# A full-row low part for the attention scores, and the convolution's shifted products all on VectorE

## The chip, the cores and the metric

One core of a Trainium2 chip runs the whole program. The metric is the device time of one execution in microseconds (us), the median of several runs. The engines are named as the profile names them: PE (TensorE matmul), PEld (its weight loads), DVE (VectorE), ACT (ScalarE), POOL (GpSimd), SP (SyncE, which issues most DMAs).

## The reference, cut to what matters

The reference is two transformer blocks in float32 over 1024 tokens of width 1024. Only two pieces of the first block are touched by the change. One is a causal depthwise convolution of width 31 over 256 channels; the other is a differential attention with 4 heads, each with two maps of 64 dimensions.

```python
u = a_val * jax.nn.sigmoid(a_gate)                       # 1024 x 256
y = conv_general_dilated(u, w_dw, padding=[(30, 0)], feature_group_count=256) + b_dw
y = silu(layer_norm(y)) @ w_pw + b_pw
...
q, k = rms_norm(q.reshape(.., 4, 2, 64)), rms_norm(k.reshape(.., 4, 2, 64))
s = einsum("bhmqd,bhmkd->bhmqk", q, k) * scale - slope * dist   # both maps m, causal
p = softmax(s)
o = einsum("bhqk,bhkd->bhqd", p[:, :, 0] - lam * p[:, :, 1], v)
```

After it come an output projection, a mixture of experts and two more layers, which the change leaves as they are.

## The kernel before, in words

Matrix products work on float32 values split into a high and a low part (`wh`, `wl` for weights, `mh`, `ml` for activations), and add three of the four partial products. A weight granule arrives by DMA in `raw` (4 buffers), ACT copies it to `wh` (L451), and `low` (L443) makes `wl`: two of three such splits go to DVE, the third to POOL (L447). Large tiles share one pool of 42 buffers, matmul results of one PSUM bank share 4 (`mm`), and the score tiles share 2 (`sc`).

The order of work on each engine follows the order in which Python generators are stepped. `_weave(main, side, steps)` takes one step of `main`, then `steps` steps of `side`. Each engine runs its own list in order, so an instruction that is traced early stands ahead of later ones on its engine. A scheduler may move an instruction behind others that it takes to be ready earlier.

The first block's stages, in order of time:

- `conv_pool`: the products for the convolution's values, its gate and the pooling input. It has 24 steps; 13 are run first, and the other 11 are the second half of the tokens (`psT`).
- `qkv`: 8 steps for V (`psV`, 24 matmuls of 512 columns each), then 24 steps for Q and K (`psQ`), in four column groups of six steps. Each Q or K tile goes through ACT (L792), DVE (`qss` L794, `qn` L797), a PE transpose, and a copy and subtraction (L813, L814). The first group's weights `wl` are split at the end of the V steps.
- `diff_attention`: 32 units (head, block of 128 queries), with scores `psD` on PE, maximum on DVE (L897), exponentials on ACT (L902), scaling on POOL (L907), combination on DVE (L908), transposes on PE (L918), then the product with V (`psO`).

`conv_taps(half)` does the 31 shifted multiply-adds of the convolution for one half of the tokens and for both channel groups `j`, in 31 steps. DVE adds all shifts of group 0 and 18 of group 1 in place (L664), 96 instructions in all. For 12 shifts of group 1, ACT makes the product (L672) and POOL adds it to a third tile `ys[2]` (L673), which POOL adds to `ys[1]` at the end (L675). Half 0 is woven into the last 11 steps of `conv_pool` at 2.6 steps each. Half 1 is the first part of the side chain of `qkv`, at 3 steps for one; `pool_out` (24 steps, with 6 wide adds on POOL, L687, and four subtractions on DVE, L693) and `conv_norm` (20 steps) come behind it in the chain.

For the scores, `k[m][h]` holds the high part of map `m` on one half of the partitions and its low part on the other half. `query_maps(h)` copies the high part of the query of each map to both partition halves, with three DMAs of 256 KB on POOL's queue: two for the tile `qh2` (L848), one in place that waits for them (L849). The matmul `high` (L876) takes 128 rows: high query with both parts of the key. The matmul `low` (L880) takes only 64 rows: low query with the high key. They follow each other in pairs, one pair for each block of at most 512 keys.

Of the kernel before, what the change touches and what calls it, by code (L numbers as in the profile page):

```python
# [10 lines left out]
F32R = mybir.dt.float32r  # L11
I32 = mybir.dt.int32
U8 = mybir.dt.uint8
AF = mybir.ActivationFunctionType
OP = mybir.AluOpType
# [242 lines left out]
def _run(g):  # L258
    for _ in g:
        pass  # L260


def _weave(main, side, steps=1.0):

    due = 0.0
    for _ in main:
        yield
        due += steps
        while due >= 1.0:
            due -= 1.0  # L270
            if next(side, _END) is not _END:
                yield
    yield from side


def _some(gen, n):

    for _ in range(n):
        if next(gen, _END) is _END:
            return  # L280
        yield


def _chain(*gens):
    for g in gens:
        yield from g
# [31 lines left out]
class _Kernel:  # L318
# [321 lines left out]
        yield from self.group(lead, [  # L640
            lambda t0, n, j=j, use=use: self.partT(("c", j), self.hm, use, t0, n=n) for j, use in enumerate(uses)])

    def conv_taps(self, half):

        nc = self.nc
        us = self.us
        if half == 0:
            self.ys = [self.d("cy") for _ in range(3)]
        ys = self.ys
        n2 = 12  # L650
        lo, hi = 512 * half, 512 * half + 512
        for j in range(2):
            nc.vector.tensor_scalar(ys[j][:, lo:hi], us[j][:, lo:hi], self.col(("cw", j), 30), self.col("cb", j),
                                    op0=OP.mult, op1=OP.add)
        if half == 0:
            nc.gpsimd.memset(ys[2][:, 0:hi], 0.0)
        else:
            nc.scalar.activation(ys[2][:, lo:hi], us[1][:, lo - 30:hi - 30], AF.Copy, scale=self.col(("cw", 1), 0))
        yield
        last = 31 if half == 0 else 30  # L660
        for sh in range(1, 31):
            a = max(lo, sh)
            for j in range(2 if sh <= 30 - n2 else 1):
                nc.vector.scalar_tensor_tensor(ys[j][:, a:hi], us[j][:, a - sh:hi - sh], self.col(("cw", j), 30 - sh),  # L664
                                               ys[j][:, a:hi], op0=OP.mult, op1=OP.add)
            n = last + n2 - 31
            if sh * n // 30 > (sh - 1) * n // 30:
                s2 = last - sh * n // 30
                a = max(lo, s2)
                p = self.t512("cpr")[:, :hi - a]  # L670
                with self.tc.issue_after(self.evicted.ins):
                    nc.scalar.activation(p, us[1][:, a - s2:hi - s2], AF.Copy, scale=self.col(("cw", 1), 30 - s2))  # L672
                nc.gpsimd.tensor_tensor(ys[2][:, a:hi], ys[2][:, a:hi], p, op=OP.add)  # L673
            yield
        nc.gpsimd.tensor_tensor(ys[1][:, lo:hi], ys[1][:, lo:hi], ys[2][:, lo:hi], op=OP.add)  # L675

    def pool_out(self):
        nc = self.nc
# [163 lines left out]

    def query_maps(self, h):

        a = self.q[0][h]
        b = self.d("qh2", dt=F32R)
        for r in (slice(0, 64), slice(64, 128)):
            self.nc.gpsimd.dma_start(b[r], a[64:128])  # L848
        self.nc.gpsimd.dma_start(a[64:128], a[0:64])  # L849
        self.q2[h] = [a, b]  # L850

    def diff_attention(self):
        nc = self.nc
# [5 lines left out]
        def unit(h, i):  # L859
# [11 lines left out]
            qa = slice(128 * i, 128 * i + 128)  # L871
            pd = {}
            blocks = [slice(c0, min(w, c0 + 512)) for c0 in range(0, w, 512)]

            def high(m, b):
                nc.tensor.matmul(pd[m][:, b], self.q2[h][m][:, qa], self.k[m][h][:, b], start=True, stop=False)  # L876

            def low(m, b):
                r = slice(64 * m, 64 * m + 64)
                nc.tensor.matmul(pd[m][:, b], self.q[1][h][r, qa], self.k[m][h][r, b], start=False, stop=True)  # L880
            for m in range(2):
                if w > 512:
                    pd[m] = self.sc("psD")
                elif m == 0:
                    both = self.sc("psD", (128, 2, 512))
                    pd = [both[:, 0], both[:, 1]]
                for b in blocks:
                    high(m, b)
                    low(m, b)
                ps = pd[m]  # L890
                if w > 512:
                    t = self.d("at")
                else:
                    if m == 0:
                        two = self.d("at", (128, 2, 512))
                    t = two[:, m]
                nc.vector.tensor_tensor_reduce(t[:, :w], ps[:, :w], bias[:, 896 - 128 * i:896 - 128 * i + w],  # L897
                                               1.0, -3.0e38, OP.add, OP.max, mx[:, m:m + 1])
                tt.append(t)
            nc.vector.tensor_scalar(nm, mx, -slope, None, op0=OP.mult)  # L900
            for m in range(2):
# [7 lines left out]
                                           op0=OP.mult, op1=OP.add)  # L909
# [20 lines left out]
            if i ^ 1 in done[h]:  # L930
                c0 = 256 * (i // 2)
                b = slice(c0, c0 + 256)
                r = q = self.t256("ar")
# [11 lines left out]
                if len(done[h]) == NT:  # L945
                    self.q[0][h] = self.q[1][h] = self.k[0][h] = self.k[1][h] = self.q2[h] = None
                yield
        yield from _pipe(unit(h, i) for h, i in ATTN_ORDER)
        self.q = self.k = self.v = None

# [1189 lines left out]
    def build(self):  # L2140
        nc = self.nc
# [26 lines left out]
        first = self.conv_pool(lead)  # L2168
        _run(_some(first, 6))
        self.lambdas()  # L2170
        _run(_some(first, 7))
        _run(_weave(first, self.conv_taps(0), 2.6))
        self.ahead = 1
        _run(_weave(self.qkv(), _chain(self.conv_taps(1), self.pool_out(), self.conv_norm()), 3))
        if self.stop == "qkv":
            return
        self.ahead = 0
# [15 lines left out]
        def products():  # L2193
            self.pre(8)
            for half, t in self.out_proj(("o1",), self.io["x"], self.after_first, order, fill, True):
                if (half, t) == (1, order[5]):
                    self.rope_tables()
                    self.make_masks()
                if (half, t) == (0, order[6]):
                    self.choose_most()  # L2200
                if (half, t) == (1, order[-1]):
                    self.ple_load(0)
                    self.pre(1)
                if (half, t) == (0, order[-1]):
                    _run(_some(side, 1))
                yield
# [75 lines left out]
```

## Time and profile before

| | |
|---|---|
| median of 3 runs | 2355.36 us (2348.99 to 2358.8) |
| the profiled execution | 2339.19 us, span 2337.4 us |
| mean granted TensorE clock in it | 0.97 |
| PE busy | 93% of the span |
| DVE busy | 65% |
| ACT busy | 50% |
| POOL busy | 23% |

The profiled execution is a single one and a little shorter than the three timed runs. Its span is the time between its first and last instruction; some 2 us lie around it. Busy shares are means over stages with different limits, and a matmul's recorded time overlaps that of its neighbours: the distance between two starts says what one costs in a row.

### The profile page before, as it was taken

The page shows a single profiled execution, that of the slowest core. Times are in us where ns is not written, and L with a number is a line of the kernel's source. Part 1 is how long each engine was busy: PE and PEld are TensorE (multiplying, and loading weights), DVE is VectorE, ACT ScalarE, POOL GpSimd, SP SyncE. Part 2 cuts the span into 40 slices and gives each one's busy share as a digit, 9 for nine tenths or more (in the row PEclk, how much of TensorE's full clock was granted, in tenths as well). Part 3 has the DMA queues.
Part 4 walks back from the last instruction along what each step waited for, and adds up shares of the span by engine and source line. Part 5 has one row for each costly group of instructions (what it writes and reads, how often), then busy time and mean ns, then how long its engine had stood idle before and what let it go on. Part 6 is the DMA issues. An engine that isn't in the chain of part 4 may idle for free.

```text
span 2337.4 us, 31235 instructions
## 1 busy us (share of the span) xinstructions
PE 2182.8 (93%) x11660; PEld 1822.4 (78%) x11660; DVE 1515.9 (65%) x2574; ACT 1171.0 (50%) x2216; POOL 531.2 (23%) x445
## 2 busy tenths in 40 slices
PE   7869999999999889988899999999998989999998
PEld 7659866787777768877687998888877777898886
DVE  5995677667777744567736775476167675676455
ACT  5414666525666656254344564266345444555344
POOL 1740033302222211012232342011012232233110
PEclk9889999999999999999999999999999999999999
DMA  5101210537899973011122014344001102103343
GB/s 202 36 1 52 80 46 24 173 117 265 241 289 317 306 224 121 10 37 46 46 81 55 19 46 162 127 181 139 27 28 41 68 30 75 42 28 126 126 154 126
DMA packets 77487, 251.95 MB, mean 108 GB/s; under 512 B 9488, under 2 KB 16784, under 8 KB 77328
## 3 DMA queue, kind: packets, MB, share of 16 engines
q1 hardware_dynamic: 65024, 205.84, 25.4%
q0 software_dynamic: 9712, 34.86, 6.3%
q10 hardware_dynamic: 2592, 9.18, 1.0%
q8 instruction: 94, 1.54, 0.3%
q14 instruction: 65, 0.53, 0.1%
HBM read 183.51 MB, written 58.98 MB: 104 GB/s over the span
## 4 chain that ended last, share of the span: by engine, by line
PE 65%; DVE 18%; ACT 6%; DMA 6%; issue 4%; POOL 1%; SPq 0%; DVEq 0%; ACTq 0%; POOLq 0%
PE psR L501 18%; PE psT L470 11%; PE psS L460 6%; PE psO L460 5%; PE psV L501 4%; DMA raw<-in_wm_dram 4%; PE psQ L501 3%; DVE cy L664 3%; PE psG L1309 2%; DVE wl L447 2%; PE psPT L1937 2%; PE psY L460 2%; DVE st L1702 2%; DVE st L1705 2%; PE psD L880 1%
## 5 line engine op out<-in xcount | busy, mean ns | idle before, releaser
L470 PE MATMUL psT<-mh,wh 128*128 128x512 f32 (+1 forms) x784 | 291.6, 372 | 10.2 <-ACT k L1570 4.4
L447 DVE TENSOR_TENSOR wl<-raw,wh 128x1024 fp32r<-128x1024 f32 x171 | 226.8, 1338 | 104.3 <-ACT wh L451 102.9
L470 PE MATMUL psT<-ml,wh 128*128 128x512 f32 (+1 forms) x784 | 288.5, 368 | 2.1 <-DVE ml L559 2.1
L470 PE MATMUL psT<-mh,wl 128*128 128x512 f32 (+1 forms) x784 | 287.2, 367 | 0.0
L451 ACT ACTIVATE wh<-raw 128x1024 fp32r<-128x1024 f32 x205 | 213.8, 1055 | 62.9 <-DMA raw<-in_wm_dram 40.5
L447 POOL TENSOR_TENSOR wl<-raw,wh 128x1024 fp32r<-128x1024 f32 x34 | 98.5, 2896 | 405.0 <-ACT wh L451 306.2
L470 PEld LDWEIGHTS psT<-mh,wh 128*128 128x128 f32 x784 | 152.6, 195 | 37.8 <-ACT k L1570 5.1
L470 PEld LDWEIGHTS psT<-ml,wh 128*128 128x128 f32 x784 | 152.8, 195 | 25.2 <-DVE ml L559 2.9
L470 PEld LDWEIGHTS psT<-mh,wl 128*128 128x128 f32 x784 | 152.5, 194 | 22.9 <-issue 0.2
L501 PE MATMUL psR<-wh,mixh 128*128 128x512 f32 x384 | 152.9, 398 | 2.7 <-DVE mpT L1942 1.7
L501 PE MATMUL psR<-wh,mixl 128*128 128x512 f32 x384 | 150.4, 392 | 0.6 <-POOL mixl L447 0.5
L501 PE MATMUL psR<-wl,mixh 128*128 128x512 f32 x384 | 150.4, 392 | 0.0
L1925 POOL TENSOR_SCALAR mp<-mp,mrr 128x512 f32<-128x512 f32 x128 | 92.1, 732 | 213.3 <-DVE mrr L1923 213.3
L1921 ACT ACTIVATE mp<-psS,mnm,rq 128x1024 f32<-128x1024 f32 x64 | 77.4, 1209 | 82.5 <-DVE mnm L1918 82.4
L501 PE MATMUL psR<-wl,mh 128*128 128x512 f32 (+1 forms) x264 | 101.3, 384 | 1.2 <-DVE wl L447 1.2
L501 PE MATMUL psR<-wh,mh 128*128 128x512 f32 (+1 forms) x264 | 102.0, 386 | 0.0
L501 PE MATMUL psR<-wh,ml 128*128 128x512 f32 (+1 forms) x264 | 101.1, 383 | 0.0
L558 ACT ACTIVATE mh<-psX 128x256 fp32r<-128x256 f32 (+1 forms) x144 | 60.8, 452 | 77.4 <-PE psX L550 72.2
L460 PEld LDWEIGHTS psO<-mpT,mv 128*128 128x128 f32 x768 | 96.4, 191 | 2.6
L1916 DVE TENSOR_REDUCE mmx<-psS 128x1 f32<-128x1024 f32 x64 | 78.0, 1219 | 29.7 <-PE psS L460 29.5
L460 PE MATMUL psO<-mpT,mv 128*128 128x256 f32 x768 | 97.1, 283 | 0.0
L664 DVE SCALAR_TENSOR_TENSOR cy<-u,cols,cy 128x512 f32<-128x512 f32 (+28 forms) x96 | 95.9, 1059 | 0.4
(496 smaller groups left out, 5723.6 us busy)
## 6 DMA issues: line engine op xcount, KB each, us to landing
raw<-in_wg_dram SPq DMA_DIRECT2D x109, 512.0 KB, 3.9
raw<-in_wm_dram SPq DMA_DIRECT2D x96, 512.0 KB, 5.3
pp<-ppo ACTq DMA_DIRECT2D x16, 512.0 KB, 7.0
h<-xr SPq DMA_DIRECT2D x16, 512.0 KB, 2.9
xr<-h SPq DMA_DIRECT2D x16, 512.0 KB, 4.4
ppr<-pp SPq DMA_DIRECT2D x16, 512.0 KB, 5.6
xt<-in_x_dram SPq DMA_DIRECT2D x8, 512.0 KB
xr<-in_x_dram SPq DMA_DIRECT2D x8, 512.0 KB, 5.0
```

The costliest lines, as they stand in the source:

```text
L447: e.tensor_tensor(out, full, high.bitcast(F32), op=OP.subtract)
L451: self.nc.scalar.activation(h, src, AF.Copy)
L460: self.nc.tensor.matmul(out, a, b, start=j == 0, stop=j == n - 1)
L470: self.nc.tensor.matmul(ps, p[:, a], q, start=k == 0 and j == 0, stop=k == nk - 1 and j == 2)
L501: self.nc.tensor.matmul(out, p, q[:, b], start=k == 0 and j == 0, stop=k == 7 and j == 2)
L558: nc.scalar.activation(h, v, AF.Copy)
L664: nc.vector.scalar_tensor_tensor(ys[j][:, a:hi], us[j][:, a - sh:hi - sh], self.col(("cw", j), 30 - sh), ys[j][:, a:hi], op0=OP.mult, op1= ...
L1309: self.nc.tensor.matmul(pg, m[x][:, k], w[:, b], start=k == 0 and n == 0, stop=k == 7 and n == 2)
L1702: nc.vector.scalar_tensor_tensor(st[(c + 1) // 8][0:64, (c + 1) % 8], st[c // 8][0:64, c % 8], er[0:64, 1, c:c + 1], ds[c % 2][0:64, c // ...
L1916: nc.vector.tensor_reduce(mx, ps, axis=AX.X, op=OP.max)
L1921: nc.scalar.activation(p, ps, AF.Exp, bias=nm, scale=self.rq[0][:, t:t + 1], accum_out=sm)
L1925: nc.gpsimd.tensor_scalar(p[:, b], p[:, b], rr, 1.0, op0=OP.mult, op1=OP.mult)
```

## The change

`conv_taps` becomes one generator for both halves. DVE does all shifted products of both groups; the products on ACT, the additions on POOL and the third tile are gone. Only 14 of its 62 steps are woven into `conv_pool`, at 1.3 for one. The other 48 are woven with `pool_out` (0.55 steps of it for one of taps), and that, followed by `conv_norm`, is woven into `qkv` at 3.4 for one.

`query_maps` now also copies the low part of the query to both partition halves, with three more DMAs and one more tile per head. The second score matmul becomes one of 128 rows: low query with both parts of the key.

```diff
-    def conv_taps(self, half):
+    def conv_taps(self):
...
-        n2 = 12
...
-            for j in range(2 if sh <= 30 - n2 else 1):
-                nc.vector.scalar_tensor_tensor(ys[j][:, a:hi], us[j][:, a - sh:hi - sh], self.col(("cw", j), 30 - sh),
-                                               ys[j][:, a:hi], op0=OP.mult, op1=OP.add)
-            n = last + n2 - 31
-            if sh * n // 30 > (sh - 1) * n // 30:
...
-                    nc.scalar.activation(p, us[1][:, a - s2:hi - s2], AF.Copy, scale=self.col(("cw", 1), 30 - s2))
-                nc.gpsimd.tensor_tensor(ys[2][:, a:hi], ys[2][:, a:hi], p, op=OP.add)
...
+        ys = self.ys = [self.d("cy") for _ in range(2)]
+        for half in range(2):
...
+            for sh in range(1, 31):
+                a = max(lo, sh)
+                for j in range(2):
+                    nc.vector.scalar_tensor_tensor(ys[j][:, a:hi], us[j][:, a - sh:hi - sh], self.col(("cw", j), 30 - sh),
+                                                   ys[j][:, a:hi], op0=OP.mult, op1=OP.add)
+                yield
...
-        a = self.q[0][h]
-        b = self.d("qh2", dt=F32R)
-        for r in (slice(0, 64), slice(64, 128)):
-            self.nc.gpsimd.dma_start(b[r], a[64:128])
-        self.nc.gpsimd.dma_start(a[64:128], a[0:64])
-        self.q2[h] = [a, b]
+        self.q2[h] = [[], []]
+        for n in range(2):
+            a = self.q[n][h]
+            b = self.d("qh2", dt=F32R)
+            for r in (slice(0, 64), slice(64, 128)):
+                self.nc.gpsimd.dma_start(b[r], a[64:128])
+            self.nc.gpsimd.dma_start(a[64:128], a[0:64])
+            for m, t in enumerate((a, b)):
+                self.q2[h][m].append(t)
...
-            def low(m, b):
-                r = slice(64 * m, 64 * m + 64)
-                nc.tensor.matmul(pd[m][:, b], self.q[1][h][r, qa], self.k[m][h][r, b], start=False, stop=True)
+            def products(m, b):
+
+                for n in range(2):
+                    nc.tensor.matmul(pd[m][:, b], self.q2[h][m][n][:, qa], self.k[m][h][:, b], start=n == 0, stop=n == 1)
...
-        _run(_weave(first, self.conv_taps(0), 2.6))
+        taps = self.conv_taps()
+        _run(_weave(first, _some(taps, 14), 1.3))
         self.ahead = 1
-        _run(_weave(self.qkv(), _chain(self.conv_taps(1), self.pool_out(), self.conv_norm()), 3))
+        _run(_weave(self.qkv(), _chain(_weave(taps, self.pool_out(), 0.55), self.conv_norm()), 3.4))
```

## Rows read from the trace of the kernel before

**Rows 1.** The page: busy time of TensorE, its share and instructions.

```profile
PE 2182.8 (93%) x11660; PEld 1822.4 (78%) x11660; DVE 1515.9 (65%) x2574; ACT 1171.0 (50%) x2216; POOL 531.2 (23%) x445
```

**Rows 2.** Windows by stage: start:end, length; busy of PE, PEld, DVE, ACT, POOL; PEclk.

```profile
97.00:150.50 53.50, 48.04 (x197) 38.65 (x195) 53.50 (x52) 18.44 (x28) 30.74 (x19) 0.90 0.09 30
150.50:174.30 23.80, 1.50 (x14) 1.30 (x12) 23.41 (x18) 0.44 (x1) 16.45 (x13) 0.60 0.00 0
174.30:240.00 65.70, 63.15 (x472) 59.65 (x473) 35.47 (x71) 31.75 (x82) 4.79 (x2) 0.96 0.19 65
240.00:289.50 49.50, 47.41 (x374) 44.77 (x374) 34.87 (x70) 36.86 (x88) 4.93 (x5) 1.00 0.24 70
289.50:425.00 135.50, 132.17 (x673) 91.67 (x671) 102.25 (x303) 93.39 (x241) 43.40 (x60) 0.97 0.12 31
```

**Rows 3.** Waits, 56 to 180 us: total, times, longest.

```profile
PE psQ L501 <- DVE wl L447: 22.3, 1, 22.3
...
PE psV L501 <- DVE wl L447: 5.5, 2, 3.2
```

**Rows 4.** Timeline of PE in the V steps: start, duration.

```profile
97.19 0.39 PE L501 MATMUL psV<-wh,ml 128*128 128x512 f32 x1
...
99.46 0.39 PE L501 MATMUL psV<-wl,mh 128*128 128x512 f32 x1
...
109.40 0.63 PE L501 MATMUL psV<-wh,ml 128*128 128x512 f32 x1
...
112.39 0.63 PE L501 MATMUL psV<-wl,mh 128*128 128x512 f32 x1
```

**Rows 5.** Windows, the shifted products (L664) alone: length, DVE busy (count), PEclk.

```profile
65.00:81.00 16.00, 15.16 (x23) 0.96 0.00 0
115.00:129.00 14.00, 14.00 (x9) 1.00 0.01 2
...
154.50:170.00 15.50, 15.25 (x8) 0.52 0.00 0
```

**Rows 6.** Timeline of POOL, the additions of half 1: start, time.

```profile
110.87 18.05 POOL L673 TENSOR_TENSOR cy<-cy,cpr 128x512 f32<-128x512 f32 x11
```

**Rows 7.** Lines, DVE from 174.3 to 289.5 us: busy us, mean ns.

```profile
L794 DVE TENSOR_REDUCE qss<-qsq 128x4 f32<-128x256 f32 x31 | 12.9, 417 | 23.2 <-ACT qsq L792 23.0
L447 DVE TENSOR_TENSOR wl<-raw,wh 128x1024 fp32r<-128x1024 f32 x6 | 9.2, 1536 | 2.7 <-ACT wh L451 2.7
L814 DVE SCALAR_TENSOR_TENSOR ql<-psQT,qg,qh 128x256 fp32r<-128x256 f32 x16 | 7.7, 481 | 1.6 <-ACT qh L813 1.2
...
L693 DVE SCALAR_TENSOR_TENSOR pd<-ps,pin 64x1008 f32<-64x1008 f32 x4 | 4.8, 1198 | 0.1
```

**Rows 8.** Timeline of PE in the attention: start, duration.

```profile
323.08 0.47 PE L876 MATMUL psD<-qh 128*128 128x512 f32 x1
323.49 0.49 PE L880 MATMUL psD<-qh,ql 64*128 64x512 f32 x1
323.91 0.38 PE L876 MATMUL psD<-ql,qh 128*128 128x256 f32 x1
```

**Rows 9.** One of the four groups of score matmuls: min/median/max ns, shapes.

```profile
L880 PE MATMUL psD<-qh,ql x48: 323/491/792, 289.9 to 416.3; 64*128 64x512 f32 x24, 64*128 64x384 f32 x8, 64*128 64x256 f32 x8, 64*128 64x128 f32 x8
```

**Rows 10.** Waits, 292 to 430 us: total, times, longest.

```profile
DVE at L897 <- PE psD L880: 19.8, 23, 2.5
...
DVE at L908 <- POOL at L907: 6.2, 9, 1.5
...
DVE few L905 <- ACT at L902: 2.6, 3, 1.2
...
DVE at L920 <- PE psAT L918: 2.2, 2, 2.0
```

**Rows 11.** Timeline of POOL: the query copies of head 0.

```profile
275.31 1.09 POOL L848 DMA_DIRECT2D qh<-qh  x2 [13.30 <-PE psQ L501]
...
282.33 0.51 POOL L849 DMA_DIRECT2D qh<-qh  x1 [4.97 <-DVE qn L797]
```

More of the change, by code (lines that the diff above doesn't have):

```diff
@@ L641, in conv_pool @@
             lambda t0, n, j=j, use=use: self.partT(("c", j), self.hm, use, t0, n=n) for j, use in enumerate(uses)])
-    def conv_taps(self, half):
+    def conv_taps(self):
         nc = self.nc
         us = self.us
-        if half == 0:
-            self.ys = [self.d("cy") for _ in range(3)]
-        ys = self.ys
-        n2 = 12
[L651 to L662, printed above, removed]
-            for j in range(2 if sh <= 30 - n2 else 1):
-                nc.vector.scalar_tensor_tensor(ys[j][:, a:hi], us[j][:, a - sh:hi - sh], self.col(("cw", j), 30 - sh),
-                                               ys[j][:, a:hi], op0=OP.mult, op1=OP.add)
-            n = last + n2 - 31
-            if sh * n // 30 > (sh - 1) * n // 30:
[L668 to L671, printed above, removed]
-                    nc.scalar.activation(p, us[1][:, a - s2:hi - s2], AF.Copy, scale=self.col(("cw", 1), 30 - s2))
-                nc.gpsimd.tensor_tensor(ys[2][:, a:hi], ys[2][:, a:hi], p, op=OP.add)
-            yield
-        nc.gpsimd.tensor_tensor(ys[1][:, lo:hi], ys[1][:, lo:hi], ys[2][:, lo:hi], op=OP.add)
@@ new lines, in conv_taps @@
+        ys = self.ys = [self.d("cy") for _ in range(2)]
+        for half in range(2):
+            lo, hi = 512 * half, 512 * half + 512
+            for j in range(2):
+                nc.vector.tensor_scalar(ys[j][:, lo:hi], us[j][:, lo:hi], self.col(("cw", j), 30), self.col("cb", j),
+                                        op0=OP.mult, op1=OP.add)
+            yield
+            for sh in range(1, 31):
+                a = max(lo, sh)
+                for j in range(2):
+                    nc.vector.scalar_tensor_tensor(ys[j][:, a:hi], us[j][:, a - sh:hi - sh], self.col(("cw", j), 30 - sh),
+                                                   ys[j][:, a:hi], op0=OP.mult, op1=OP.add)
+                yield
@@ L873, in unit @@
             blocks = [slice(c0, min(w, c0 + 512)) for c0 in range(0, w, 512)]
-            def high(m, b):
-                nc.tensor.matmul(pd[m][:, b], self.q2[h][m][:, qa], self.k[m][h][:, b], start=True, stop=False)
-            def low(m, b):
-                r = slice(64 * m, 64 * m + 64)
-                nc.tensor.matmul(pd[m][:, b], self.q[1][h][r, qa], self.k[m][h][r, b], start=False, stop=True)
+            def products(m, b):
+                for n in range(2):
+                    nc.tensor.matmul(pd[m][:, b], self.q2[h][m][n][:, qa], self.k[m][h][:, b], start=n == 0, stop=n == 1)
             for m in range(2):
@@ L887, in unit @@
                 for b in blocks:
-                    high(m, b)
-                    low(m, b)
+                    products(m, b)
                 ps = pd[m]
```

## The prediction

> **What bounds the kernel now.** The page comes first: TensorE is busy for 93% of the span [rows 1], so most of the kernel is bound by PE, and work moved among the other engines is worth something only where PE waits for one of them. The windows by stage show where that is [rows 2]. From 97 us come 53.5 us for the V steps at a mean granted clock of 0.90, and 23.8 us in which PE is busy for 1.5 us while DVE is busy for 23.4. The waits name the cause [rows 3]: PE waits once for 22.3 us and twice for 5.5 us together, each time for a low weight part `wl` from DVE. The weights have been there; the split stands on DVE behind the shifted products of half 1, which were traced before it. So in this stretch DVE sets the end.
>
> The timeline of PE gives two prices [rows 4]. At full speed (2.4 GHz) a matmul of 512 columns takes (99.46 - 97.19)/10 = 0.227 us. After the waits it takes (112.39 - 109.40)/7 = 0.427 us: PE stood, and came back at the lower level of its clock (1.2 GHz).
>
> The windows with only the shifted products show why DVE is late [rows 5]. Alone, one costs 15.16/23 = 0.66 us. From 115 to 129 us one costs 14.0/9 = 1.56 us, and from 154.5 to 170 us 15.25/8 = 1.9 us. In the earlier of these POOL was adding the products of ACT to its tile, 11 additions in 18.05 us [rows 6]; in the other it ran the wide adds of `pool_out`. A product on DVE takes two to three times as long while POOL adds.
>
> In the attention PE is the bound: busy for 132 of 135.5 us, with DVE at 102, ACT at 93 and POOL at 43 [rows 2].
>
> **The taps, removed.** 24 products on ACT and 24 additions on POOL go, which by itself gains nothing, since neither engine is on the path. It takes away the slowing of [rows 5] at its first place. DVE gets 24 more products: 120 in place of 96.
>
> **The V steps.** 8 x 24 matmuls at 0.227 us are 43.6 us, against 53.5: 9.9 us are lost now, 5.5 by waiting, 4.4 by the clock. Then come the 22.3 us wait, and a restart at the lower clock: the window after it has a mean of 0.96 over 65.7 us, which is 2.6 us lost. Together 34.8 us are to be had, if DVE keeps up.
>
> Does it? After the change, the 8 V steps carry 27 side steps: 17 or 18 of taps and 9 of `pool_out`. These are 35 products at 0.66 = 23 us; eight of them run beside POOL's wide adds, as they do now, at 1.9, which adds 10. Four subtractions at 1.2 with their small parts [rows 7] are 6 us, three or four splits at 1.5 are 5. The sum is 44 us, against 43.6 of PE. DVE is full, but not behind: the split that PE waits for now should be done within a microsecond or two of when it is wanted. I take 1 us of waiting here.
>
> **The Q and K steps.** The 24 steps take 65.7 + 49.5 - 2.6 = 112.6 us. The taps last through 13 of them, 61 us of PE. DVE's own work there, by [rows 7]: in the two Q groups 32 reductions at 0.42, as many scalings that I take to be as long, and 16 subtractions at 0.48 make 21.1 us, the first step of the third group 2.4, four splits at 1.5 make 6. The remaining 59 products at 0.66 are 39 us. The sum is 68.5 us in 61: DVE is behind by 7.5 us, and PE with it, since each tile's result leaves through DVE. POOL's own splits slow some products. If no product is slowed and gaps fill perfectly, the loss is 0; with a third of the 59 products at 1.56 it is 25. I take 9, near the sum. `conv_norm` follows in the last steps, where DVE has room: 70 of 115 us are busy now.
>
> So the first part brings 34.8 - 1 - 9 = 25 us.
>
> **The score products.** The timeline of PE in the attention [rows 8] has the next start 0.41 us after a high matmul of 512 columns begins, and 0.42 us after a low one. In the V steps 512 columns take 0.227. So each change between 128 and 64 rows costs some 0.19 us, in both directions. There are four groups of 48 such matmuls [rows 9], so 192 x 0.19 = 36 us of the stage's 135.5 are this change-over. Both products of all 128 rows take it away. The row alone doesn't say that the row count is the reason; it could be the narrow stream itself, which the new form has too, and then the gain is 0. Against this, the high product, which already has 128 rows, pays the same as the low one, so the price goes with the change and not with the form. I take 36.
>
> The Trainium skill has a rule for each reading. TensorEngine Tiling (Array Packing), section Key Properties, says that changing the tiling mode drains TensorE; by it the 36 us go. TensorE: Matmul & The Clock Gate, section "Why this matters for your kernels", says that a single matmul of 32 rows takes the same time as one of 128; read by itself, it makes the new low products as long as the old ones, and the gain would be 0. The trace agrees with the first.
>
> PE then has some 99.5 us of work in the attention, and DVE with 102 becomes the bound. The stage can't go below 102 (a gain of 33). Of DVE's present idle time, 19.8 us are waits for PE's scores and 6.2 for POOL [rows 10]. The wait for POOL and those for ACT and for the transposes, 2.6 and 2.2, stay, and of the 19.8 a third may, as two score buffers leave little room. That gives 102 + 6 + 5 + 3 = 116 us, a gain of 19. If every wait stayed it would be 0.
>
> **The query copies.** 12 more DMAs of 0.55 us on POOL are hidden for the later heads: POOL is busy for 43 of 135.5 us there, and the copies are asked for six units ahead. What is queued behind a waiting one is POOL's scaling (L907), for which DVE waits. For head 0 there is little time: the two copies are sent at 275.3 us, the one in place at 282.3 [rows 11], and the first scores start near 290 [rows 9]. A second set wholly behind the first would be 7 us later, and its last copy lands after the scores want it. Between 0 and 7 us; I take 1, as POOL did other work between the copies and the second pair need not wait for the third transfer.
>
> **The sum.** 2339.2 - 25 - 19 + 1 = 2296 us for the profiled execution. The runs' median is 1.0069 times that execution, so the forecast for it is 2312 us. Half a per cent, 12 us, is about what this measurement can tell from no change.
>
> **The rivals.**
>
> - *The score matmuls don't get shorter.* If the narrow stream costs the 0.19 us, only the first part remains: 2355 - 24 = 2331. For it speaks that no pair of 128 rows of this form is in the trace; against it, the equal price in both directions. I give it 0.12. The rule of the Trainium skill on the row count (TensorE: Matmul & The Clock Gate, above) would make this the case.
> - *DVE is too full in the Q steps.* With 25 us lost there in place of 9, the first part brings 9 and the whole 27: 2328. For it: 68.5 us of work in 61. Against it: POOL is busy for only 4.8 us of the 65.7 in this window now. 0.13.
> - *Both of these.* 2355 - 9 + 1, some 2347: no change. 0.08.
> - *Both parts better.* DVE's gaps fill, and the attention falls to 104: 34 + 31 us, 2290. 0.10.
> - *Slower: the taps ahead of `qss` and `qn`.* Each Q tile's way out of PSUM stands on DVE behind four or five products. With p us for one product, the 13 steps take 59p + 29.5 us on DVE against 61 on PE. The whole gain of 34.8 + 19 is gone at p = 1.45. At 1.9, the price beside POOL's wide adds, they take 142 us, 81 too many, and the kernel comes to 2355 + 27 = 2382. It would need POOL reading in most of these 61 us, where now it has two splits. 0.05.
> - The forecast itself has 0.52, with 2300 to 2324 as its own range.
>
> Faster by over 0.5%: 0.52 + 0.12 + 0.13 + 0.10 = 0.87; within: 0.08; slower: 0.05. The range from 2288 to 2338 takes in the forecast and the rivals at 2290, 2328 and 2331.
>
> **What would show it.** The step on the V weights is right if PE's wait for `wl` at the end of the V steps is under 3 us and its clock stays at 1.0. The price of a tap is right if products take 0.7 us or less outside `pool_out`. The step on the Q steps is right if PE's idle time between V and attention is near 10 us, with DVE named. The score step is right if `psD` starts stand 0.23 us apart for 512 columns, and the attention ends up with PE waiting for DVE (L897). The forecast is wrong if the distances stay at 0.4, if DVE's products cost over 1 us in the Q steps, or if PE's new gaps in the attention send its clock to the lower level and so give the gain back.

## The result, and the profile after

The changed kernel takes 2318.03 us (median of 4 runs, 2313.66 to 2323.02), the kernel before, run beside it, 2353.62 (4 runs, 2348.99 to 2358.8). The ratio is 0.984, with a 95% interval from 0.982 to 0.986: faster by 1.6%, some 36 us where 43 were forecast, inside the range of 2288 to 2338. A second series of the same kernel (the first experiment below) gave 2314.11 us and a ratio of 0.985 (0.982 to 0.987).

The profiled execution of the changed kernel took 2323.02 us. The busy times of its page, to be read against [rows 1]:

```profile
PE 2165.4 (93%) x11660; PEld 1831.0 (79%) x11660; DVE 1510.8 (65%) x2598; ACT 1156.0 (50%) x2192; POOL 499.7 (22%) x431
```

The shares say as little as before. The stages are in the windows (start:end and length; busy of PE, PEld, DVE, ACT, POOL; granted clock of PE; DMA share and GB/s), to be read against [rows 2]:

```profile
95.20:138.80 43.60, 43.60 (x194) 36.13 (x193) 43.49 (x56) 6.69 (x10) 23.39 (x11) 1.00 0.00 1
138.80:152.40 13.60, 3.18 (x22) 2.94 (x21) 13.57 (x21) 0.60 (x1) 0.00 (x0) 0.74 0.02 4
152.40:182.00 29.60, 25.75 (x191) 24.51 (x190) 29.21 (x51) 9.70 (x32) 2.74 (x1) 0.90 0.10 35
182.00:240.00 58.00, 57.38 (x433) 54.57 (x433) 28.98 (x56) 32.27 (x80) 4.77 (x2) 0.96 0.17 55
240.00:274.00 34.00, 29.46 (x219) 26.42 (x218) 27.07 (x55) 27.67 (x65) 4.21 (x7) 1.00 0.48 124
274.00:396.60 122.60, 106.87 (x673) 91.67 (x673) 105.86 (x306) 93.85 (x244) 48.94 (x69) 0.96 0.23 55
```

The V steps now take 43.6 us, all of it PE at full clock; before, 53.5 at 0.90. The stretch in which PE mostly stands and DVE is full has shrunk from 23.8 us to 13.6, and has not gone. DVE is full without a break from 95 to 182 us, and half idle from 182 to 240. In the attention no engine is full any longer.

The waits from 95 to 275 us (total, times, longest) name the rest of the first part; with [rows 3], PE's three waits for `wl` have become one:

```profile
PE psQ L501 <- DVE wl L447: 10.4, 1, 10.4
...
PE psQT L788 <- DVE qn L781: 5.2, 5, 2.0
```

After that wait PE comes back at the lower level of its clock (1.2 GHz), as it did in [rows 4]: the starts of 256 columns stand 0.21 us apart up to 155.6 us, and 0.12 from there on, in PE's timeline (start, duration):

```profile
151.97 0.41 PE L501 MATMUL psQ<-wl,mh 128*128 128x256 f32 x1
152.18 0.41 PE L501 MATMUL psQ<-wh,mh 128*128 128x256 f32 x1
```

Windows with the shifted products (L657) alone answer to [rows 5] (length, DVE busy and count, clock, DMA):

```profile
65.00:82.00 17.00, 16.96 (x23) 1.00 0.09 31
95.00:105.00 10.00, 10.00 (x7) 1.00 0.00 0
105.00:120.00 15.00, 13.87 (x23) 1.00 0.00 1
...
129.40:148.70 19.30, 19.30 (x29) 0.92 0.00 0
152.40:182.00 29.60, 21.34 (x27) 0.90 0.10 35
```

Away from POOL's wide sums a product costs 0.60 to 0.74 us up to 149 us, and 0.79 in the Q steps (the last line). From 95 to 105 us, beside the sums, it costs 1.43. From 120 to 128 other instructions hold DVE: the first terms of half 1 (L651, one for each channel group) take 2.56 us together, and a product of 16 columns (L680) takes 2.35. POOL suffers as well. Its timeline (start, duration) has a copy of four columns that takes 6.34 us, where one of two takes 0.5; the last line is DVE's at that time:

```profile
95.86 0.52 POOL L670 COPY ps<-ps 128x2 f32<-128x2 f32 x1
96.34 2.39 POOL L671 TENSOR_TENSOR ps<-ps 128x1022 f32<-128x1022 f32 x1
...
114.11 6.34 POOL L670 COPY ps<-ps 128x4 f32<-128x4 f32 x1 [9.53 <-DVE pf L680]
120.41 2.19 POOL L671 TENSOR_TENSOR ps<-ps 128x1020 f32<-128x1020 f32 x1
```

```profile
114.62 5.78 DVE L657 SCALAR_TENSOR_TENSOR cy<-u,cols,cy 128x486 f32<-128x486 f32 x9
```

The copy ends at 120.45 us, when these nine products have ended (120.40). Of the two first terms, the second takes 2.10 us and ends at 122.88, just behind the sum of 120.41. I read this as one engine standing until the other has done, and not as both at a lower rate; no run isolates it.

In the attention, PE's timeline shows what the score product has become; with [rows 8]:

```profile
288.39 0.39 PE L865 MATMUL psD<-qh 128*128 128x512 f32 x1
288.61 0.39 PE L865 MATMUL psD<-qh,ql 128*128 128x512 f32 x1
288.84 0.28 PE L865 MATMUL psD<-qh 128*128 128x256 f32 x1
```

The starts of 512 columns stand 0.22 to 0.23 us apart, where they stood 0.41 and 0.42. The waits of this stretch, to be read against [rows 10] (L865 are the scores, L881 the maximum on DVE, L892 the combination, L902 the transposes; `at` and `few` are tiles that DVE writes):

```profile
PE psAT L902 <- DVE at L892: 4.7, 7, 2.1
PE psD L865 <- DVE few L881: 4.7, 6, 2.5
...
DVE at L881 <- PE psD L865: 3.4, 5, 1.2
```

DVE's wait for scores has gone from 19.8 to 3.4 us, and now PE waits for DVE. So three dates tell the story of a run: the start of V (95.4 us; 97.0 before), the first score product (274.06; 289.5), and the first product of the output projection, which ends the attention (396.6; 427.3). The last two, from the views of `psD` and `psR` (count, min/median/max ns, first and last start, shapes), of the kernel before and then of the changed one:

```profile
L876 PE MATMUL psD<-qh x48: 305/455/774, 289.5 to 416.0; 128*128 128x512 f32 x24, 128*128 128x384 f32 x8, 128*128 128x256 f32 x8, 128*128 128x128 f32 x8
L501 PE MATMUL psR<-wh,mixh x384: 387/389/775, 427.3 to 2237.1; 128*128 128x512 f32 x192
```

```profile
L865 PE MATMUL psD<-qh x48: 221/416/795, 274.1 to 384.4; 128*128 128x512 f32 x24, 128*128 128x384 f32 x8, 128*128 128x256 f32 x8, 128*128 128x128 f32 x8
L501 PE MATMUL psR<-wh,mixh x384: 387/389/586, 396.6 to 2220.9; 128*128 128x512 f32 x192
```

Of 30.7 us won up to there, 15.4 lie ahead of the first score product (1.6 of them ahead of V) and 15.3 in the attention.

### The profile page after: what moved, and what is told of

The parts are those of the page before. It is cut to its first block, busy times and chain, and to the rows that moved or that the text cites. A ratio compares the mean times of both kernels' runs of the same rounds, so it can differ in the third digit from the quotient of the medians.

```text
span 2321.2 us, 31232 instructions
## 1 busy us (share of the span) xinstructions
PE 2165.4 (93%) x11660; PEld 1831.0 (79%) x11660; DVE 1510.8 (65%) x2598; ACT 1156.0 (50%) x2192; POOL 499.7 (22%) x431
## 4 chain that ended last, share of the span: by engine, by line
PE 47%; DVE 10%; ACT 4%; issue 3%; DMA 1%; POOL 0%; ACTq 0%; DVEq 0%; POOLq 0%; SPq 0%
PE psR L501 14%; PE psT L470 10%; PE psS L460 6%; PE psO L460 4%; PE psV L501 4%; PE psPT L1921 2%; DVE st L1686 2%; DVE st L1689 2%; PE psO L1700 1%; PE psO L1697 1%; PE psMV L460 1%; PE psA L1662 1%; PE psX L550 1%; DVE wl L447 1%; DVE B L1633 1%
## 5 line engine op out<-in xcount | busy, mean ns | idle before, releaser
L470 PE MATMUL psT<-ml,wh 128*128 128x512 f32 (+1 forms) x784 | 289.5, 370 | 2.1 <-DVE ml L559 2.1
L447 POOL TENSOR_TENSOR wl<-raw,wh 128x1024 fp32r<-128x1024 f32 x34 | 88.8, 2611 | 454.9 <-ACT wh L451 391.5
L470 PEld LDWEIGHTS psT<-ml,wh 128*128 128x128 f32 x784 | 153.3, 195 | 25.5 <-DVE ml L559 2.5
L501 PE MATMUL psR<-wh,mixl 128*128 128x512 f32 x384 | 149.9, 390 | 0.9 <-POOL mixl L447 0.9
L460 PEld LDWEIGHTS psO<-mpT,mv 128*128 128x128 f32 x768 | 96.4, 191 | 2.6
L460 PE MATMUL psO<-mpT,mv 128*128 128x256 f32 x768 | 97.1, 283 | 0.0
L988 DVE TENSOR_TENSOR xr<-psR,xr 128x512 f32<-128x512 f32 x48 | 33.1, 691 | 93.9 <-PE psR L501 83.9
```

Of the source, the lines that this page charges most:

```text
L447: e.tensor_tensor(out, full, high.bitcast(F32), op=OP.subtract)
L460: self.nc.tensor.matmul(out, a, b, start=j == 0, stop=j == n - 1)
L470: self.nc.tensor.matmul(ps, p[:, a], q, start=k == 0 and j == 0, stop=k == nk - 1 and j == 2)
L501: self.nc.tensor.matmul(out, p, q[:, b], start=k == 0 and j == 0, stop=k == 7 and j == 2)
```

## The experiments

**The same kernel again.** No edit.

> The changed kernel itself, as the measure for the run with the early split on the same chip: ratio to the kernel before 0.982 to 0.986, some 2318 us; a profile without the lower clock at 1760 to 1840 us would have its last output product near 2296 us, not 2311.

It took 2314.11 us. Its profiled execution has the first score product at 275.6 and the end of the attention at 398.3, within 2 us of the first one; but from there to the last matmul it takes 1897 us, where the first took 1914 (and the kernel before 1900). The code of that stretch is the same. What differs is the clock. One window of 40 us, of the first and then of this one:

```profile
1740.00:1780.00 40.00, 36.99 (x198) 31.80 (x197) 21.98 (x47) 11.72 (x16) 2.57 (x2) 0.83 0.04 14
```

```profile
1740.00:1780.00 40.00, 36.99 (x213) 30.90 (x212) 26.78 (x55) 20.73 (x29) 6.11 (x3) 1.00 0.10 37
```

PE is equally busy in both, at a mean clock of 0.83 and of 1.00. By the starts of the same matmuls, the first execution falls 6 us behind from 1750 to 1786 us, 4.5 from 951 to 985 (0.87 against 1.00 from 945 to 985) and 4.4 from 1815 to 1849 (0.86 from 1800 to 1850, against 0.97 from 1790 to 1840): 15 of the 17 us. So the profiled pair differs by only 16 us where the medians differ by 36, and the three dates are the better measure of the change. They have a noise of their own: in the four profiles with the changed convolution and no other edit to it (these two, the new convolution alone, and the transposed probabilities on ACT) the first score product starts between 273.0 and 275.6 us.

**The new scores alone.** The kernel before, with the new `query_maps` and score products only.

> The convolution stays as before; only the score products and the query copies are changed. Theory (each change between 128 and 64 rows costs TensorE 0.19 us): score matmuls of 512 columns stand 0.23 us apart, the stretch from the first score product to the first product of the output projection goes from 137.8 us to 121 to 126, the time falls by 12 to 17 us (ratio 0.993 to 0.995). Rival (the attention only looked shorter after the change because its start came at another state of DVE, the taps are the whole gain): the stretch stays above 133 us, ratio 0.998 or more.

2335.94 us, ratio 0.993 (0.991 to 0.996). PE's wait of 22.3 us for `wl` stands as before; the attention lasts from 290.7 to 414.2, 123.5 us.

**The new convolution alone.** The changed kernel, with `query_maps` and the score products of before.

> Only the convolution is changed; the low score products keep their 64 rows. Theory (the two parts are independent and add up): first score product at 274 us in place of 289.5, the stretch to the output projection stays at 136 to 139 us, the time falls by 14 to 21 us (ratio 0.991 to 0.994), and with the run of the score products alone it makes the 36 us of the whole change. Rival (the parts overlap, both take from the same wait): the two falls make 45 us or more together, or less than 27.

2328.93 us, ratio 0.991 (0.988 to 0.994). The first score product starts at 273.0, and the attention takes 137.7 us, as before (137.8). Against 2351.07 us of the kernel before in the same series, the two parts bring 15.1 and 22.1 us; both of them together, in the run above, 37.0. They add up, as far as it can be told: each ratio is known to 0.3%, some 7 us.

**The split of the first Q weights earlier.**

```diff
         grans = [self.w(("v1", 0, kq)) for kq in range(4)]
+        self.pre(1)
         for t in range(NT):
```

> The changed kernel, with the second weight granule of the first Q group asked for together with those of V, so that its split stands behind 30 shifted products on DVE, not behind 97. Theory 1 (the remaining wait of 10.4 us at the start of the Q steps is a matter of the split's place in DVE's order): this wait is under 1 us, the first score product comes 7 to 11 us earlier, 2307 to 2311 us. Theory 2 (DVE is the bound from 64 to 182 us, and PE waits there as long for something else): first score product at most 3 us earlier, 2315 to 2318 us.

2317.87 us, ratio 0.986 (0.983 to 0.989), and the first score product at 275.1: no gain. In the order of instructions on DVE, 97 of the 124 products and first terms stand ahead of the two splits that PE waits for; now 30 stand ahead of one of them and 96 ahead of the other. PE's wait for `wl` is gone, and this has come in its place (PE's waits, 95 to 275 us; `qn` was 5.2 us; here as in later edits the line numbers have moved by one or two):

```profile
PE psQT L789 <- DVE qn L782: 15.0, 7, 6.8
```

So the wait for `wl` is only where DVE's lateness shows. What is late is DVE as a whole.

**The products held in the order in which they are woven.** A scheduler may move instructions ahead; here those from the 15th step on keep their place on DVE.

```diff
+                    with self.queued(mybir.EngineType.DVE) if half or sh > 13 else ExitStack():
                         nc.vector.scalar_tensor_tensor(ys[j][:, a:hi], us[j][:, a - sh:hi - sh], self.col(("cw", j), 30 - sh),
```

> The changed kernel, with the shifted products from the 15th step on held in the order of the weave on DVE, so that 64 of them stand ahead of the weight split that PE waits for, not 97. Theory 1 (the prediction's sum of DVE's work was right, its place in the order was not): the wait for the split is under 2 us, the products last until about 195 us, first score product at 264 to 268 us in place of 275, 7 to 10 us off the time of the changed kernel. Theory 2 (DVE's work between 95 and 182 us is the bound whatever its order): PE's waits turn up behind qn in the Q steps, and the first score product stays within 3 us of 275.

2320.67 us, ratio 0.988 (0.985 to 0.991), the first score product at 277.9: a little worse. The windows show why (columns as above):

```profile
105.00:139.00 34.00, 34.00 (x152) 28.15 (x151) 26.75 (x36) 5.49 (x8) 6.38 (x4) 1.00 0.05 13
...
182.00:220.00 38.00, 31.70 (x221) 29.15 (x220) 33.18 (x56) 14.86 (x41) 2.54 (x1) 0.91 0.12 42
220.00:240.00 20.00, 16.06 (x108) 15.07 (x107) 11.47 (x24) 8.94 (x24) 0.05 (x1) 0.83 0.00 1
```

64 products now stand ahead of the splits, in place of 97, and PE's wait for `wl` is 0.8 us. But DVE now stands idle for 7 of 34 us in the V steps, products last to 240 us, and PE waits for `qn` in the Q steps (7.8 and 4.4 us) and loses clock there. An even spread, which was thought to help, moves the loss, as the second theory had it.

This is also the nearest that a run comes to the order on which the prediction's sum rests. 30 products and first terms stand between the start of V and the split, where 35 were counted, and 60 products are left for the Q steps, where 59 were. DVE's groups from 139 to 241 us have these (busy us, mean ns):

```profile
L658 DVE SCALAR_TENSOR_TENSOR cy<-u,cols,cy 128x512 f32<-128x512 f32 x60 | 47.3, 852 | 0.0
```

That is 0.79 us each. From the start of V (95.4) to the first score product (277.9) 182.5 us pass.

**The wide sums of `pool_out` on DVE.**

```diff
-                nc.gpsimd.tensor_copy(nxt[:, 0:sh], cur[:, 0:sh])
-                nc.gpsimd.tensor_tensor(nxt[:, sh:], cur[:, sh:], cur[:, :S - sh], op=OP.add)
+                nc.scalar.activation(nxt[:, 0:sh], cur[:, 0:sh], AF.Copy)
+                nc.vector.tensor_tensor(nxt[:, sh:], cur[:, sh:], cur[:, :S - sh], op=OP.add)
```

> The changed kernel, with the six wide additions of the pooling sums on DVE in place of POOL and their short copies on ACT. Theory (an addition on POOL that reads beside DVE's products costs DVE as much as doing it itself): products cost 0.66 to 0.70 us everywhere from 95 us on, where seven took 10 us beside POOL's additions; DVE gains some 9 us and gives 7 for the six additions; 88 products stand ahead of the split, its wait falls from 10.4 to 2 to 6 us; first score product 0 to 4 us earlier, the time equal within 4 us. Rival (the slow products are not POOL's doing): DVE has 7 us more to do, the wait grows, first score product 3 to 7 us later.

2308.23 us, ratio 0.981 (0.978 to 0.984). DVE has been given more work, and the first score product comes at 264.0, 10 us earlier, more than the theory had. The wait for `wl` is 1.0 us. But 88 products instead of 97 now stand ahead of the split, so the order may have a part in it.

**`pool_out` behind all the products.** The sums stay on POOL.

```diff
-        _run(_weave(self.qkv(), _chain(_weave(taps, self.pool_out(), 0.55), self.conv_norm()), 3.4))
+        _run(_weave(self.qkv(), _chain(taps, self.pool_out(), self.conv_norm()), 3.4))
```

> The changed kernel, with pool_out behind all the shifted products in place of woven among them; the six wide sums stay on POOL. It tells apart whether the sums' meeting with the products is what cost in the V and Q steps, or the products' number. Theory 1 (the meeting costs): the products ahead of the V steps' end cost 0.60 to 0.70 us each (1.43 in 95 to 105 us in the changed kernel), PE's wait for the Q weights wl falls from 10.4 us to under 4, and the first score product starts at 264 to 269 us in place of 274; median 2308 to 2314. Theory 2 (the sums cost the same wherever they stand): they then meet the Q steps' own work on DVE (reductions, scalings, subtractions of 0.4 to 0.5 us become 0.7 to 1.2), and the first score product starts at 272 to 277; median 2315 to 2320, the same as the changed kernel.

2321.17 us, ratio 0.988 (0.985 to 0.991), the first score product at 278.5. Neither expectation holds as a whole. The products cost 0.62 us (10.00 us for 16 from 95 to 105), and PE does not wait for `wl` any more. The time is lost again in the Q steps, and not in the way that the second theory had it. POOL's timeline, then DVE's:

```profile
192.93 0.19 POOL L670 COPY ps<-ps 128x2 f32<-128x2 f32 x1 [29.60 <-PE psQ L501]
193.07 1.89 POOL L671 TENSOR_TENSOR ps<-ps 128x1022 f32<-128x1022 f32 x1
```

```profile
194.99 1.21 DVE L677 SCALAR_TENSOR_TENSOR pd<-ps,pin 64x1008 f32<-64x1008 f32 x1 [4.34 <-POOL ps L671]
...
198.01 0.42 DVE L778 TENSOR_REDUCE qss<-qsq 128x4 f32<-128x256 f32 x1
```

POOL stands for 29.6 us until a `psQ` matmul, which I read as a wait for a buffer that PE still reads. Its second sum comes so late that DVE's subtraction (L677) waits for it, and behind that, in DVE's queue, stand the reductions and scalings of the Q tiles, for which PE waits.

**Without the wide sums.** The six sums and their short copies are left out, so that the order on DVE stays that of the changed kernel, with 97 products ahead of the split.

> The changed kernel without pool_out's six wide sums and their short copies: that part of the computation (the windowed sums of the pooling branch) is left out, the rest stands in the same order on VectorE, 97 shifted products ahead of the split of the first Q weights, as in the changed kernel. It tells apart what brought the first score product from 274 to 264 us when the sums went to VectorE: that products no longer meet POOL's sums, or that 88 instead of 97 products then stood ahead of the split. Theory 1 (the meeting): in 95.2 to 149.9 us of the changed kernel some 10 us of VectorE's time are slowing (62 products at 0.75 instead of 0.67, 3 small ones at 0.9 instead of 0.16, 2 starts at 1.3 instead of 0.5); without the sums PE's wait of 10.4 us falls under 2, and the first score product starts at 261 to 266 us; median 2304 to 2311. Theory 2 (the order): the wait stays over 7 us and the first score product starts at 270 to 275; median 2313 to 2318.

2306.11 us, ratio 0.981 (0.978 to 0.983), and the first score product at 263.5. The groups of DVE from 95.2 us on, in the changed kernel up to its split (149.9), and here up to 142 (busy us, mean ns | idle before):

```profile
L657 DVE SCALAR_TENSOR_TENSOR cy<-u,cols,cy 128x512 f32<-128x512 f32 (+15 forms) x62 | 47.5, 837 | 0.1
...
L680 DVE TENSOR_TENSOR pf<-ps,sm 64x16 f32<-64x16 f32 x3 | 2.7, 893 | 0.0
L651 DVE TENSOR_SCALAR cy<-u,cols 128x512 f32<-128x512 f32 x2 | 2.6, 1319 | 0.0
```

```profile
L657 DVE SCALAR_TENSOR_TENSOR cy<-u,cols,cy 128x512 f32<-128x512 f32 (+14 forms) x61 | 40.0, 735 | 0.0
...
L651 DVE TENSOR_SCALAR cy<-u,cols 128x512 f32<-128x512 f32 x2 | 1.0, 542 | 0.0
```

At 40.0/61 = 0.656 us, 62 products would take 40.7: they are 6.8 us slower beside the sums. The two first terms are 1.6 slower, and the three small products (L680) 2.2 (0.5 us with the sums on DVE). That is 10.6 us in all, and with them go 9.4 of the 10.4 us of waiting for `wl` (PE's waits):

```profile
PE psQ L501 <- DVE wl L447: 1.0, 1, 1.0
```

The order and DVE's work were the same, so it was the meeting of DVE and POOL.

**Sums on DVE and the split earlier**, both edits as above.

> The changed kernel with the six wide sums on VectorE and the short copies on ACT, and one granule of the first Q weights split 58 products earlier (30 products ahead of it, not 88). Theory 1 (what remains in the first part is VectorE's work, whatever its order): first score product at 263 to 266 us, as with the sums on VectorE alone (264.0). Theory 2 (the order still costs): 260 us or less.

The single execution took 2304.1 us, with the first score product at 263.9, against 264.0 with the sums on DVE alone. The order of the split brings nothing here either.

**Both score products of 64 rows.** This asks whether it is the change of row count that costs, or the row count. Each map has its own half of the partitions.

```diff
+                r = slice(64 * m, 64 * m + 64)
-                    nc.tensor.matmul(pd[m][:, b], self.q2[h][m][n][:, qa], self.k[m][h][:, b], start=n == 0, stop=n == 1)
+                    nc.tensor.matmul(pd[m][:, b], self.q2[h][m][n][r, qa], self.k[m][h][r, b], start=n == 0, stop=n == 1)
```

> The changed kernel with both score products of 64 rows: the product of the high query with the low key is left out. Theory (only a change of the row count costs): between a pair's two products, and between pairs that follow each other, starts stand 0.23 us apart for 512 columns; 0.19 us are paid only where a pair meets a transpose or a product with V. Rival (a matmul of 64 rows is slow by itself): 0.41 us apart everywhere, as in the kernel before. A second rival, that the change of the partition half between the two maps costs too, would show 0.41 between the maps alone.

The single execution took 2318.7 us. PE's timeline:

```profile
309.53 0.49 PE L866 MATMUL psD<-qh 64*128 64x512 f32 x1
309.86 0.39 PE L866 MATMUL psD<-qh,ql 64*128 64x512 f32 x1
310.09 0.34 PE L866 MATMUL psD<-qh 64*128 64x384 f32 x1
310.27 0.33 PE L866 MATMUL psD<-qh,ql 64*128 64x384 f32 x1
310.53 0.44 PE L903 MATMUL psAT<-sq,at 128*128 128x128 f32 x2
```

A second product of 64 rows and 512 columns takes 0.23 us (309.86 to 310.09), like one of 128 rows in the changed kernel. It is the change that costs. The first after a product of 128 rows takes 0.33, and the last ahead of one, 384 columns, 0.26 where the one ahead of it took 0.18. The last product of 128 rows ahead of a block of 64 pays too: in this stretch those of L460 stand 0.11 us apart, and the last one 0.205 ahead of the next score product. So some 0.1 us go on either side of a change; in [rows 8] each product is both the first and the last of its row count, and pays some 0.19.

The second rival, a price for the change of the partition half, is excluded too. Where products of the two maps meet in PE's queue, they run side by side, each at its full pace (`ql,qh` is map 1):

```profile
287.63 0.49 PE L866 MATMUL psD<-qh 64*128 64x512 f32 x1
287.64 0.49 PE L866 MATMUL psD<-ql,qh 64*128 64x512 f32 x1
287.97 0.39 PE L866 MATMUL psD<-qh,ql 64*128 64x512 f32 x1
```

As a whole the attention of this run is no measure of anything: some of its score products had moved ahead to 239.6 us, and from 272 us to its end (406.5) its mean clock was 0.89.

**The transposed probabilities on ACT.**

```diff
-                if c0:
-                    nc.vector.tensor_copy(aT[:, c0:c1], pt[:, :c1 - c0])
-                else:
-                    nc.scalar.activation(aT[:, c0:c1], pt[:, :c1 - c0], AF.Copy)
+                nc.scalar.activation(aT[:, c0:c1], pt[:, :c1 - c0], AF.Copy)
```

> The changed kernel, with the 16 copies of transposed probabilities that DVE makes (some 7.7 us in the attention) moved to ACT. Theory (DVE, busy for 106 of the 122.6 us, is now the bound of the attention): the stretch from the first score product to the output projection goes from 122.6 to 115 to 119 us. Rival (the chain through all engines and the two score buffers bounds it, or ACT at 94 us comes to be the bound): it stays at 121 to 125 us.

2313.63 us, ratio 0.984 (0.981 to 0.987); the attention takes 120.0 us. In the seven other kernels here with the changed convolution, both products at 128 rows and this copy on DVE, profiled eight times, it takes 121.1 to 122.8. DVE's 16 copies bring at most 3 us, where 4 to 8 were expected of a DVE that is the bound.

**Sums on DVE, transposed probabilities on ACT.**

> The changed kernel, with pool_out's six wide sums on DVE, its short copies on ACT, and DVE's 16 copies of the transposed probabilities on ACT. The two edits alone gave 2308.2 us (first score product at 264 us, attention 122.3 us) and 2313.6 us (attention 121 us). Theory 1 (they add up, in different stages): first score product at 264, attention 120 to 121.5 us, median 2305 to 2308. Theory 2 (in the attention the bound is the chain through all engines, and ACT's queue gets longer by the same amount): attention 122 to 123, median 2307 to 2311, not to be told from the first edit alone.

2306.94 us, ratio 0.981 (0.978 to 0.985), the first score product at 263.8, the attention 120.4 us. This window is the attention:

```profile
263.80:384.20 120.40, 104.32 (x673) 88.61 (x672) 101.80 (x289) 97.37 (x260) 50.99 (x69) 0.99 0.23 56
```

DVE is 4 us less busy than in the changed kernel and the stretch 2 us shorter, and only 1 us shorter than with the sums on DVE alone (121.5 us from date to date): DVE isn't the bound of it by itself. The medians don't tell the two theories apart. With 2304 to 2308 us, the three kernels with the sums on DVE are the fastest complete ones of this study, by their medians (the third by one execution). The intervals of the other two still touch that of the changed kernel; the date of the first score product, 264 in place of 273 to 276, is clear of it.

## Why the prediction was right, and where its sizes were off

**The price of the stalls was right.** 9.9 us were to be had in the V steps. They now take 43.6 us at a clock of 1.00, the product of 192 matmuls and 0.227 us.

**"DVE is full, but not behind" failed.** The term was 1 us of waiting at the end of the V steps; the trace has 10.4. The step counted 35 products there, by the weaving. In fact 62 products stand on DVE between the start of V and the split, 97 with the earlier ones. Held in the order of the weaving there are 64 in all, so it is the scheduler that has moved the others ahead. That this alone doesn't explain the wait is shown by the run without the sums: the same order, and the wait is 1.0 us. 61 products and the rest just fit into the V steps at 0.66 us each. The 10 us by which POOL's sums slow DVE, which the prediction had in its sum, came on top of them.

**"I take 9" for the Q steps was near in the number alone.** From the start of V to the first score product, 43.6 + 112.6 = 156.2 us were the sum without any loss; the trace has 274.06 - 95.4 = 178.7. Of the 22.5 us lost, 10.4 are the wait for `wl`; 12.1 are left for the Q steps, in which DVE is named (`qn`, 5.2 us) and the clock's mean is 0.90 for 30 us. Without the sums the whole loss is 263.5 - 95.3 - 156.2 = 12.0 us, near the 10 of the forecast. That the Q steps come near to their 9 is luck, since they were not the steps of the sum: of the 59 products that it put there, 27 were left behind the split. In the run that held the order of the weaving, 60 were left; they took 47.3 us where 39 were reckoned, and from the start of V to the first score product 182.5 - 156.2 = 26.3 us were lost, with a wait for `wl` of 0.8. So in its own order, too, the step was some 16 us too hopeful. Its count of 32 reductions and as many scalings should read 16 and 16 ([rows 7] has 31 for all four groups); the 21.1 us follow from these and are right.

So the first part of the kernel brought 15.4 us in place of 25, and 25.5 with the meeting of DVE and POOL taken away (289.5 to 264.0, with the sums on DVE). The reason, a DVE that is too full in these steps, was the second rival's; it put 25 us of loss into the Q steps alone, and 22.5 came, nearly half of them ahead of the Q steps. No run separates the convolution's own edits from each other (the engine, the 14 steps ahead, the weaving); `pool_out` behind the products is the only one that was undone alone.

What the 12 us of the run without the sums are made of is open. PE's waits there, from V to the first score product, name 9.8 us, 6.0 of them for `qn`, but the 112.6 us that the sum takes as free of loss hold 3.4 us of the same kind already. An earlier split did not reduce them (263.9 us, with the sums on DVE); the order of the weaving was held only with the sums on POOL.

**The score products: mechanism right, gain 15.3 for 19.** The distance fell from 0.41 to 0.23 us, as worked out, and PE's busy time in the attention from 132 to 107 us. That the change of row count costs, and not the 64 rows, is shown by the run with both at 64. The first rival (the scores don't get shorter) is excluded by that and by the 14 us that the new scores won alone. The Trainium skill says, in TensorEngine Tiling (Array Packing), section Key Properties, that changing the mode drains TensorE; the trace agrees, at some 0.1 us on either side of a change.

The step "116 us" took DVE as the bound, at 102 us and some 14 of waits. The stretch took 122.5, with DVE at 106, PE at 107 and ACT at 94, each waiting for the others. PE does wait for DVE's maximum at the end, as foretold, but to relieve DVE by 4 us brought 2 or 3. The loop through PE, DVE, ACT, POOL and back to PE, with two score tiles, is my reading of this; it was not isolated by a run with more tiles.

**The query copies cost nothing that shows.** The price was 1 us. POOL's timeline has the last copies of head 0 sent at 267.18 and 268.85, and the first score product starts at 274.06. None of PE's waits from 240 to 274 us names a DMA.

```profile
267.18 0.52 POOL L835 DMA_DIRECT2D qh<-qh  x1 [5.99 <-DMA qh<-qh]
...
268.85 0.51 POOL L835 DMA_DIRECT2D ql<-ql  x1 [0.19 <-issue]
```

**The sum.** 25 + 19 - 1 = 43 us were forecast; 15.4 + 15.3 = 30.7 stand in the profiled pair at the end of the attention, and the medians differ by 35.6 in the first series. The two errors, of 10 and 4 us, have the same sign. That the median of 2318.03 lies only 6 us from the forecast of 2312 is luck in part: the dates hold 30.7 of the 35.6 us, and the rest falls where the code is unchanged and executions differ by 17. Of the prediction's own signs, the wait for `wl` (under 3 us) failed, the clock in the V steps, the distances of 0.23 and the wait for DVE's maximum came. The price of a product held in part: 0.60 to 0.74 up to 149 us, and 0.79 in the Q steps, where the slower rival needed 1.45.

## What to carry to other kernels

Give work to the engine that feeds the bound only with a count of what will stand ahead of the awaited instruction in the built order, not in the order of the program; but where the engine as a whole is late, another order only moves the wait (`wl` to `qn` here). Then look at which other engine works at the same time: an operation that "has room" on POOL can cost DVE more than doing it there. And when one wait of a full engine has been removed, look for the next wait on the same engine before counting the gain.

## What the runs showed of the hardware

- DVE and POOL slow each other far more than either one's busy time tells. Products of 0.6 us take 1.43 beside POOL's sums; a POOL copy of four columns takes 6.34 us beside DVE's products, and a DVE instruction on 16 columns 0.89 us in the mean instead of 0.16. With DVE idle, a POOL copy of two columns takes 0.19 us. The Trainium skill (SBUF — State Buffer, section "Who interferes with whom") says that a DVE instruction with two SBUF inputs contends with a GpSimd instruction that reads SBUF; the trace agrees. Six sums of 1.2 us are 7 us on DVE; beside it on POOL they cost it 10.6.
- A matmul of 64 rows on one half of the partitions costs the same as one of 128 where its neighbours have 64 rows on that half too (0.23 us for 512 columns); at a change of the row count some 0.1 us go on either side.
- Two matmuls of 64 rows on different halves run at the same time: their starts stand 0.01 us apart at 287.63 us in the run with both products of 64 rows, and each half keeps its own pace. No kernel here was built to use it.
- Two executions of the same code can differ by 17 us over an unchanged stretch of 1900 us, 15 of them by spells of the lower clock that come at different places.
